# Context blocks after the latent-key blocks, low parts on VectorE, finished maps parked in DRAM

## The chip, the cores and the metric

The kernel runs on one core of a Trainium2 chip. The metric is the device time of one execution in microseconds (us). Five engines work side by side: TensorE (PE, with its weight loads as PEld), VectorE (DVE), ScalarE (ACT), GpSimd (POOL) and SyncE (SP), which here does nothing but issue DMA transfers. Each engine runs its own instructions in a fixed order, and waits on semaphores for the others. TensorE's clock has two levels, 1.2 and 2.4 GHz, shown as a granted clock of 0.5 and 1.0.

## The reference, cut to what matters

Two layers over 1024 latent tokens and 256 context tokens of width 1024, all in float32:

```
hx = modulate(rms_norm(x), ...);  hc = modulate(rms_norm(ctx), ...)
(a_q, a_k, a_v, a_g, b_cq, b_ckv, b_kr, b_g, c_u, c_v, c_g, d_b, d_c, d_h, d_g) = split(hx @ w_in)
... the same columns for hc @ w_in
out_a = neighbourhood_attention(...); out_b = latent attention over keys built from b_ckv, b_kr
out_c = spatial_gating(gelu(c_u), gelu(c_v)); out_d = short_conv(d_b, d_c, d_h)
x = x + g * (concat(out_a*silu(a_g), out_b*silu(b_g), out_c*silu(c_g), out_d*silu(d_g)) @ w_out)
```

The context tokens get the same in layer 0; in layer 1 they only give keys and values.

## The kernel before

**Numbers and tiles.** Every float32 operand of a matmul is cut into a high part (a cast) and a low part (original less high part, a subtraction), and a product is three matmuls: high by high, high by low, low by high. `split` makes both parts: the cast on ACT (L360), the subtraction on POOL unless told otherwise (L365). Tokens stand in chunks: 0 and 1 (512 latent columns each) and 2 (256 context columns). The input projection goes by blocks of 128 output columns. A weight block is a load of 512 KB on SP into a `wr` tile (L369), the cast into `wh`, the subtraction into `wl`. There are two buffers each of `wr`, `wh` and `wl`, so two weight blocks can be held at a time; `x` has 20 buffers of 512 columns, `o` has four.

**The value stage of layer 0** is `value_blocks`, between `first_groups` (two head groups, their maps finished there) and the paired projections. It runs the latent-key blocks `ckv_block(2)` and `(1)`, then the ten context blocks `ctx_first` (cq, ak, aq, bg, ag, two each, chunk 2 only, 24 matmuls of 256 columns each), then value tiles `av_tile`, and between these `ckv_block(0)`. All three latent-key blocks read the weights `w`, so from the first to the last of them one buffer of `wh` and of `wl` stays taken (wh516 and wl517 below). `pe.chain(True)` fixes TensorE's order to the order of the code; the scheduler that builds the program places the other engines' instructions.

**Strassen's operands.** Chunks 0 and 1 of the later projections go through `proj2`, seven products for what would be eight. It needs sums of the activations: `right_parts(i)` makes four additions on POOL (L693), `right_sums(i)` four differences on DVE (L700), each split again. For i of 2 and 3 the sums "3" and "4" go into `o` tiles, which hold the value weights `wav` until the last value tile `av_tile(3)`. `proj2` loads six to eight weight pieces of 256 KB into `x` tiles (L720) and splits them in `w_op`; two of its first three low parts are on POOL.

**Layer 1** is `paired`: blocks ak0, `ckv_block(2)`, `(1)`, `(0)`, a gate, ak1, the value tiles, then nine `proj2` (cg, dc, dh, db, dg, cq, ak, aq, bg and ag behind).

**After the projections** keys and queries that were written to DRAM (`scr_...`) are read back on POOL's queue and attention runs. The maps (`map_(fc, c)`, `x` tiles) are gated head outputs; numbers 4 to 7 are finished early, wait out attention in SBUF, and are read when the output is merged.

Of the kernel before, what the change touches and what calls it, by code (L numbers as in the profile page):

```python
# [13 lines left out]
ALU = mybir.AluOpType  # L14
# [5 lines left out]
SEQ = 1024  # L20
CTX = 256
TOK = SEQ + CTX
# [74 lines left out]
def backbone(ctx: ExitStack, tc: tile.TileContext, a, yT, dbg=None):  # L97
# [85 lines left out]
    def f(ap):  # L183
        return ap.bitcast(F32)
# [170 lines left out]
                dve.tensor_scalar(m["G"][:, fb, :nc_], pc[:, i, :nc_], v[:, V_BM + 16 + fb:V_BM + 17 + fb], None, ALU.add)  # L355


    def split(hi, lo, raw, hi_eng="act", lo_eng="pool"):
        if hi_eng == "act":
            act.copy(hi, raw)  # L360
        elif hi_eng == "pool":
            pool.tensor_scalar(hi, raw, 1.0, None, ALU.mult)  # L362
        else:
            dve.tensor_copy(hi, raw)
        (pool if lo_eng == "pool" else dve).tensor_tensor(lo, raw, f(hi), ALU.subtract)  # L365

    def w_load(src):
        raw = T("wr", [1024])
# [3 lines left out]
    def w_block(src, scale=None, raw=None, **k):  # L372
        if raw is None:
            raw = w_load(src)
        hi, lo = T("wh", [1024], F32R), T("wl", [1024], F32R)
        if scale is None:
            split(hi, lo, raw, **k)
        else:
            act.activation(hi, raw, AF.Copy, scale=scale)
            dve.scalar_tensor_tensor(lo, raw, scale, f(hi), ALU.mult, ALU.subtract)  # L380
        return hi.rearrange("p (k n) -> p k n", k=8), lo.rearrange("p (k n) -> p k n", k=8)
# [40 lines left out]
    def layer(l, H):  # L422
        last = l == DEPTH - 1
        v = vecs[l]
# [6 lines left out]
        def htok(t, kc, hl):  # L431
# [7 lines left out]

        scr = {k: dr.tile(s, F32, name=f"scr_{k}{l}", tag=f"scr_{k}{l}") for k, s in  # L440
               (("cq", [2, 256, TOK]), ("ck", [2, 128, TOK]), ("kr", [2, 64, TOK]), ("k", [2, 256, TOK]),
                ("q", [2, 256, TOK]), ("v", [TOK, 256]), ("vw", [4, 512, 256]))}

        M = {}

        def map_(fc, c):

            if c < 2:
                if (fc, c) not in M:
                    M[fc, c] = T("x", [512])  # L450
                return M[fc, c]
            if (fc // 2, 2) not in M:
                M[fc // 2, 2] = T("x", [2, 256])
            return M[fc // 2, 2][:, fc % 2, :]

        all_chunks = (0, 1, 2) if not last else (0, 1)

# [74 lines left out]
        ahead_w = {}  # L532
# [155 lines left out]
        def right_parts(i):  # L688

            t = {}  # L690
            for k, (c, kc) in enumerate(((0, i), (1, i), (1, i + 4), (0, i + 4))):
                t[k] = T("x", [512])
                pool.tensor_tensor(t[k], f(H[c, kc][:, 0, :]), f(H[c, kc][:, 1, :]), ALU.add)  # L693
            R["11", i], R["21", i], R["22", i] = H[0, i], H[0, i + 4], H[1, i + 4]
            return t

# [65 lines left out]
            step(6, x_, "4", False)  # L762
            evac(0, x_, 1)

        def block_c(name, c, evac):

            hi, lo = ahead_w.get(name) or w_block(a["wtb"][l, BLOCKS.index(name)])
            p = PS("b", [CHUNKS[c][1]])
            mm3(p, [(hi[:, kc, :], lo[:, kc, :], hap(c, kc, 0), hap(c, kc, 1)) for kc in range(KC)])
            evac(c, p)  # L770
# [38 lines left out]
        def value_blocks(ctx_first):  # L809

            wav = w_tok(a["wav"][l], 288, ("o", "o"), ("o", "o"))
            pe.chain(True)
            late = []

            def ckv_block(c, hi, lo):
                p = PS("b", [CHUNKS[c][1]])
                mm3(p, [(hi[:, kc, :], lo[:, kc, :], hap(c, kc, 0), hap(c, kc, 1)) for kc in range(KC)])
                late.append(ckv_steps(c, p))

            def on():  # L820
                for fn in [fns.pop(0) for fns in late if fns]:
                    fn()

            w = w_block(a["wtb"][l, BLOCKS.index("ckv0")])
            ckv_block(2, *w)
            ckv_block(1, *w)
            for name, fn in ctx_first:
                block_c(name, 2, fn)
                on()
            for t in (8, 9):  # L830
                av_tile(t, wav)
            ckv_block(0, *w)
            parts = [right_parts(0), right_parts(1)]
            for i in range(2):
                right_sums(i, parts[i])
            for t in (4, 5, 6, 7):
                av_tile(t, wav)
                on()
            for i in range(2, 4):
                right_sums(i, right_parts(i))  # L840
            for t in range(4):
                av_tile(t, wav)
            pe.chain(False)
            av_windows()

        def half_paired():
            first_groups()
            while fillers:
                fillers.pop(0)()
            evacs = {"cq": cq_evac, "ak": k_evac, "aq": lambda c, p, j: q_evac(c, p, j, 0.125),  # L850
                     "bg": lambda c, p, j: act.activation(map_(2 + j, c), p, AF.Silu),
                     "ag": lambda c, p, j: act.activation(map_(j, c), p, AF.Silu)}
            value_blocks([(f"{n}{j}", lambda c, p, n=n, j=j: evacs[n](c, p, j)) for n in evacs for j in range(2)])
            proj2("cq", evacs["cq"])
            kr = kr_rotate()
            proj2("ak", k_evac)
            kr_transpose(*kr)
            proj2("aq", evacs["aq"])
            cq_stats()
            w_tags.remove("wr")  # L860
            proj2("bg", evacs["bg"])

        def paired():
            wav = w_tok(a["wav"][l], 288, ("o", "o"), ("o", "o"))
            pe.chain(True)
            block_c("ak0", 2, lambda c, p: k_evac(c, p, 0))
            late = []

            def ckv_block(c, hi, lo):
                p = PS("b", [CHUNKS[c][1]])  # L870
                mm3(p, [(hi[:, kc, :], lo[:, kc, :], hap(c, kc, 0), hap(c, kc, 1)) for kc in range(KC)])
                for fn in [fns.pop(0) for fns in late if fns]:
                    fn()
                late.append(ckv_steps(c, p))

            w = ahead_w["ckv0"]
            ckv_block(2, *w)
            ckv_block(1, *w)
            ckv_block(0, *w)
            cv_gate(0)  # L880
            parts = [right_parts(0)]
            block_c("ak1", 2, lambda c, p: k_evac(c, p, 1))
            for fns in late[1:]:
                fns.pop(0)()
            av_tile(8, wav)
            late[-1].pop()()
            parts.append(right_parts(1))
            for t in (9, 4):
                av_tile(t, wav)
            cv_gate(1)  # L890
            for i in range(2):
                right_sums(i, parts[i])
            for t in (5, 6, 7):
                av_tile(t, wav)
            for i in range(2, 4):
                right_sums(i, right_parts(i))
            for t in range(4):
                av_tile(t, wav)
            pe.chain(False)
            av_windows()  # L900
            proj2("cg", lambda c, p, j: gate(c, p, 4 + j))
            proj2("dc", lambda c, p, j: act.copy(map_(6 + j, c), p))
            kr = kr_rotate()
            z = {}

            def conv_in(c, p, j):
                z[j, c] = T("x", [512])
                dve.tensor_tensor(z[j, c], p, map_(6 + j, c), ALU.mult)

            proj2("dh", conv_in)  # L910
            kr_transpose(*kr)
            for j in range(2):
                w = [v[:, V_SC + 3 * j + i:V_SC + 3 * j + i + 1] for i in range(3)]
                for c in range(2):
                    m = map_(6 + j, c)
                    act.activation(m, z[j, c], AF.Copy, scale=w[1])
                    for d, s_, k in ((m[:, 1:], z[j, c][:, :511], 0), (m[:, :511], z[j, c][:, 1:], 2),
                                     (m[:, 0:1], z[j, 0][:, 511:], 0) if c else (m[:, 511:], z[j, 1][:, 0:1], 2)):
                        dve.scalar_tensor_tensor(d, s_, w[k], d, ALU.mult, ALU.add)

            def mulb(c, p, j):
                m = map_(6 + j, c)
                dve.tensor_tensor(m, p, m, ALU.mult)

            proj2("db", mulb)
            proj2("dg", lambda c, p, j: gate(c, p, 6 + j))
            proj2("cq", cq_evac)
            proj2("ak", k_evac)
            proj2("aq", lambda c, p, j: q_evac(c, p, j, 0.125))
            cq_stats()  # L930
            w_tags.remove("wr")
            proj2("bg", lambda c, p, j: act.activation(map_(2 + j, c), p, AF.Silu))
# [543 lines left out]
        units[0].prep()  # L1476
        pe.chain(False)
        ph.close()
        ph = Phase("att", ("pt", "pc"))
        queue, ends = [], []  # L1480
        for u, un in enumerate(units):
# [203 lines left out]
```

## Time and profile before

| | |
|---|---|
| median of three runs | 1534.22 us (1533.8 to 1536.93) |
| the profiled execution, its own time | 1531.37 us |
| its span in the trace | 1529.6 us |
| TensorE busy | 1404.1 us, 92% of the span |
| VectorE, ScalarE, GpSimd busy | 947.6, 645.2, 567.6 us |
| moved by DMA | 171.70 MB, mean 112 GB/s |

The busy times of the engines lie side by side; with TensorE at 92% what can be gained or lost is where TensorE stands still or runs at its lower clock. Durations below come from this one execution.

### The profile page before, as it was taken

What the parts mean: (1) busy time and instruction counts of PE and PEld (TensorE: products, weight loads), DVE (VectorE), ACT (ScalarE), POOL (GpSimd) and SP (SyncE); (2) the same over time, 40 slices, a digit from 0 to 9 for tenths busy, and PEclk for the clock granted to TensorE, in tenths of its full rate; (3) what the DMA queues carried; (4) which work ended last, traced back from release to release, by engine and by line L of the source; (5) the groups of instructions that cost most, each with busy time, mean ns of one, the idle gap of its engine ahead of it and who ended that gap; (6) DMA issues with size and microseconds to landing.
All of it is one profiled execution on the core that took longest, in us unless ns stands there. A gap on an engine that the chain in (4) does not pass through costs nothing. (4 is left out here: it accounts for less than half of the span.)

```text
span 1529.6 us, 23255 instructions
## 1 busy us (share of the span) xinstructions
PE 1404.1 (92%) x8784; PEld 1176.0 (77%) x8784; DVE 947.6 (62%) x1999; ACT 645.2 (42%) x1438; POOL 567.6 (37%) x449
## 2 busy tenths in 40 slices
PE   4999999669899899999999979899999899999997
PEld 2888888559687687778888969777787678778887
DVE  5857886254554777666446564838364677765564
ACT  5612012223344666655334322433334566654543
POOL 2153354374425000245551175643434101055651
PEclk9999999769899999999999989999999999999999
DMA  9513445302457200585343112412245503285232
GB/s 354 194 49 125 138 124 176 122 20 86 165 170 171 27 1 22 134 176 144 126 151 126 57 37 81 149 46 69 69 152 154 108 1 76 80 176 144 91 129 74
DMA packets 86703, 171.70 MB, mean 112 GB/s; under 512 B 8768, under 2 KB 35392, under 8 KB 86464
## 3 DMA queue, kind: packets, MB, share of 16 engines
q1 hardware_dynamic: 69568, 141.91, 28.4%
q0 software_dynamic: 15936, 27.27, 9.2%
q8 instruction: 69, 1.13, 0.3%
q10 hardware_dynamic: 1088, 1.05, 0.2%
q14 instruction: 42, 0.34, 0.1%
HBM read 140.57 MB, written 33.82 MB: 114 GB/s over the span
## 5 line engine op out<-in xcount | busy, mean ns | idle before, releaser
L173 PE MATMUL psb<-g,wh 128*128 128x512 f32 (+1 forms) x1886 | 510.1, 371 | 16.6 <-ACT wh L360 11.1
L173 PE MATMUL psb<-g,wl 128*128 128x512 f32 (+1 forms) x1144 | 373.4, 379 | 44.3 <-POOL wl L365 36.2
L173 PEld LDWEIGHTS psb<-g,wh 128*128 128x128 f32 x1886 | 346.0, 197 | 83.0 <-ACT wh L360 14.2
L173 PEld LDWEIGHTS psb<-g,wl 128*128 128x128 f32 x1144 | 224.8, 197 | 87.5 <-POOL wl L365 39.1
L173 PE MATMUL psb<-g,st 128*128 128x512 f32 (+1 forms) x600 | 159.6, 383 | 10.4 <-ACT wl L1105 3.7
L365 POOL TENSOR_TENSOR wl<-wr,wh 128x1024 fp32r<-128x1024 f32 (+1 forms) x46 | 111.5, 2425 | 149.1 <-ACT wh L360 147.9
L1088 DVE TENSOR_REDUCE s<-psb 128x1 f32<-128x512 f32 (+1 forms) x200 | 117.5, 590 | 64.5 <-PE psb L173 62.4
L173 PE MATMUL psb<-g,g 128*128 128x256 f32 (+1 forms) x784 | 129.5, 305 | 1.8 <-ACT wh L1105 1.1
L173 PEld LDWEIGHTS psb<-g,st 128*128 128x128 f32 x600 | 95.4, 192 | 35.2 <-ACT g L1105 6.5
L173 PE MATMUL psv<-pt,g 128*64 128x256 f32 (+1 forms) x1312 | 119.4, 331 | 0.6 <-ACT pt L979 0.5
L979 ACT COPY pt<-pst 128x512 f32<-128x512 f32 x116 | 67.9, 585 | 109.5 <-PE pst L176 107.9
L173 PEld LDWEIGHTS psb<-g,g 128*128 128x128 f32 x784 | 105.4, 191 | 9.0 <-issue 2.9
L340 DVE CUSTOM_DVE_ANT_0 tmp<-g,x 128x512 f32<-128x512 f32 x112 | 96.8, 915 | 13.5 <-POOL x L474 11.8
L173 PE MATMUL psb<-g,wr 128*128 128x512 f32 (+1 forms) x490 | 98.1, 346 | 6.9 <-DMA g<-scr_cq 2.7
L173 PEld LDWEIGHTS psv<-pt,g 128*64 128x64 f32 x1312 | 79.3, 137 | 32.5 <-issue 8.6
L173 PEld LDWEIGHTS psb<-g,wr 128*128 128x128 f32 x490 | 76.9, 190 | 20.0 <-ACT wr L360 3.9
L360 ACT CAST wh<-wr 128x1024 fp32r<-128x1024 f32 (+1 forms) x41 | 40.3, 985 | 117.0 <-PE psb L173 67.9
L176 PE MATMUL pst<-ident,g 128*128 128x128 f32 x448 | 79.1, 278 | 11.3 <-ACT g L1235 6.4
L362 POOL TENSOR_SCALAR wh<-wr 128x1024 fp32r<-128x1024 f32 x16 | 44.3, 2772 | 113.1 <-PE pst L176 53.1
L977 DVE COPY pt<-pst 128x512 f32<-128x512 f32 x116 | 79.1, 683 | 6.6 <-PE pst L176 6.1
L1421 DVE SCALAR_TENSOR_TENSOR x<-psb,modG,x 128x512 f32<-128x512 f32 (+1 forms) x48 | 29.5, 615 | 85.2 <-PE psb L173 45.6
L176 PEld LDWEIGHTS pst<-ident,g 128*128 128x128 f32 x448 | 54.1, 140 | 28.0 <-ACT g L1235 8.3
(249 smaller groups left out, 2370.3 us busy)
## 6 DMA issues: line engine op xcount, KB each, us to landing
g<-in_wmod SPq DMA_DIRECT2D x48, 512.0 KB, 4.6
x<-in_wtb SPq DMA_DIRECT2D x60, 256.0 KB, 3.8
wr<-in_wtb SPq DMA_DIRECT2D x28, 512.0 KB, 3.8
wr<-in_wout SPq DMA_DIRECT2D x27, 512.0 KB, 3.6
st<-in_nab SPq DMA_DIRECT2D x24, 384.0 KB, 3.5
x<-in_xT SPq DMA_DIRECT2D x32, 256.0 KB, 5.8
g<-scr_q POOLq DMA_DIRECT2D x32, 256.0 KB, 7.3
x<-x SPq DMA_DIRECT2D x24, 256.0 KB, 2.6
```

Source lines behind the costliest of these rows:

```text
L173: return self._next(nc.tensor.matmul(*p, **k))
L176: return self._next(nc.tensor.transpose(*p, **k))
L340: dve.tensor_tensor_reduce(junk, w[:, hf * 512:hf * 512 + 512], crow[cond, hf], 1.0, 0.0, ALU.mult, ALU.add, part[:, i, cond, hf:hf + 1])
L360: act.copy(hi, raw)
L362: pool.tensor_scalar(hi, raw, 1.0, None, ALU.mult)
L365: (pool if lo_eng == "pool" else dve).tensor_tensor(lo, raw, f(hi), ALU.subtract)
L977: dve.tensor_copy(dst, src)
L979: act.copy(dst, src)
L1088: dve.reduce_max(st["mx"][:, i:i + 1], s_, AX.X)
L1421: dve.scalar_tensor_tensor(xa, p, mod[l]["G"][:, fb, cond:cond + 1], xa, ALU.mult, ALU.add)
```

## The change

In layer 0's value stage `ckv_block(0)` moves ahead of the ten context blocks; the low parts of seven of these go to DVE (two of three, the third stays on POOL); an `on()` behind the value tiles 4 to 7 goes. In layer 1 the low part of ak1 goes to DVE. `right_parts`' additions on POOL are ordered behind the last low part that the code has put on POOL so far. In both layers the finished maps 4 to 7, chunks 0 and 1, are written to DRAM (`park`, 8 transfers of 256 KB) and read back ahead of attention (`unpark`, on SP), which leaves their `x` tiles to the paired projections. The diff, cut:

```diff
     def split(hi, lo, raw, hi_eng="act", lo_eng="pool"):
...
-        (pool if lo_eng == "pool" else dve).tensor_tensor(lo, raw, f(hi), ALU.subtract)
+        m = (pool if lo_eng == "pool" else dve).tensor_tensor(lo, raw, f(hi), ALU.subtract)
+        if lo_eng == "pool":
+            last_split[0] = m
...
+        def park(fcs):
+            for fc in fcs:
+                for c in range(2):
+                    sp.dma_start(scr["m"][fc - 4, :, c * 512:(c + 1) * 512], M.pop((fc, c)))
+        def unpark():
+            for c in range(2):
+                for fc in range(4, 8):
+                    sp.dma_start(map_(fc, c), scr["m"][fc - 4, :, c * 512:(c + 1) * 512])
...
-                pool.tensor_tensor(t[k], f(H[c, kc][:, 0, :]), f(H[c, kc][:, 1, :]), ALU.add)
+                after(pool.tensor_tensor(t[k], f(H[c, kc][:, 0, :]), f(H[c, kc][:, 1, :]), ALU.add), last_split[0])
...
             ckv_block(2, *w)
             ckv_block(1, *w)
-            for name, fn in ctx_first:
-                block_c(name, 2, fn)
+            ckv_block(0, *w)
+            for n, (name, fn) in enumerate(ctx_first):
+                block_c(name, 2, fn, lo_eng=("dve", "pool")[n % 3 == 2])
                 on()
             for t in (8, 9):
                 av_tile(t, wav)
-            ckv_block(0, *w)
...
             for t in (4, 5, 6, 7):
                 av_tile(t, wav)
-                on()
...
             first_groups()
             while fillers:
                 fillers.pop(0)()
+            park((4, 5, 6, 7))
...
-            block_c("ak1", 2, lambda c, p: k_evac(c, p, 1))
+            block_c("ak1", 2, lambda c, p: k_evac(c, p, 1), lo_eng="dve")
...
             proj2("cg", lambda c, p, j: gate(c, p, 4 + j))
+            park((4, 5))
...
             proj2("dg", lambda c, p, j: gate(c, p, 6 + j))
+            park((6, 7))
...
         ph.close()
+        unpark()
```

The first place is POOL in layer 0's context blocks. In a row stand the number, the line, the operation, the tile written and those read; `wl` from a `wr` is a low part of a weight block, `x` from `g` an addition of `right_parts`, `s` a reciprocal square root. Before:

```order
66 L365 TENSOR_TENSOR wl536_2618<-wr534_2615,wh535_2617 128x1024
67 L218 TENSOR_TENSOR s540_2653<-s521_2537,mhalf_3_73 128x2
68 L218 TENSOR_TENSOR s545_2668<-s525_2567,mhalf_3_73 128x4
69 L365 TENSOR_TENSOR wl552_2688<-wr550_2685,wh551_2687 128x1024
70 L606 TENSOR_TENSOR x530_2599<-x530_2599,tmp538_2646 128x256
71 L365 TENSOR_TENSOR wl557_2723<-wr555_2720,wh556_2722 128x1024
72 L365 TENSOR_TENSOR wl562_2758<-wr560_2755,wh561_2757 128x1024
...
82 L693 TENSOR_TENSOR x603_3057<-g91_302 128x512
83 L693 TENSOR_TENSOR x604_3059<-g142_469 128x512
84 L365 TENSOR_TENSOR wl588_2930<-wr586_2927,wh587_2929 128x1024
```

and after:

```order
65 L367 TENSOR_TENSOR wl562_2750<-wr560_2747,wh561_2749 128x1024
66 L218 TENSOR_TENSOR s545_2698<-s521_2546,mhalf_3_73 128x2
67 L218 TENSOR_TENSOR s550_2713<-s525_2576,mhalf_3_73 128x4
68 L622 TENSOR_TENSOR x534_2638<-x534_2638,tmp543_2691 128x256
69 L218 TENSOR_TENSOR s555_2730<-s529_2606,mhalf_3_73 128x4
70 L367 TENSOR_TENSOR wl578_2857<-wr576_2854,wh577_2856 128x1024
71 L367 TENSOR_TENSOR wl593_2959<-wr591_2956,wh592_2958 128x1024
72 L709 TENSOR_TENSOR x604_3079<-g67_227 128x512
```

Ten low parts have become three, and no addition stands ahead of the last of them (wl588 before, wl593 after).

The second place is POOL at the end of layer 0's value stage. `o` from `x` is the low part of a sum "3" or "4"; wh658 and wl659 are low parts of the first two weight operands of `proj2("cq")`. Before:

```order
94 L693 TENSOR_TENSOR x637_3260<-g125_408 128x512
95 L365 TENSOR_TENSOR g613_3092<-x605_3061,g613_3092 128x512
96 L693 TENSOR_TENSOR x638_3262<-g159_530 128x512
97 L218 TENSOR_TENSOR s619_3159<-s597_3046,mhalf_3_73 128x4
98 L693 TENSOR_TENSOR x639_3264<-g157_525 128x512
99 L365 TENSOR_TENSOR wh658_3412<-x652_3402,wh658_3412 128x512
100 L365 TENSOR_TENSOR wl659_3415<-x653_3404,wl659_3415 128x512
101 L365 TENSOR_TENSOR o633_3247<-x629_3236,o633_3247 128x512
102 L365 TENSOR_TENSOR o635_3255<-x631_3240,o635_3255 128x512
```

and after:

```order
88 L367 TENSOR_TENSOR o633_3256<-x629_3245,o633_3256 128x512
89 L367 TENSOR_TENSOR o635_3264<-x631_3249,o635_3264 128x512
90 L709 TENSOR_TENSOR x636_3267<-g123_403 128x512
91 L709 TENSOR_TENSOR x637_3269<-g125_408 128x512
92 L709 TENSOR_TENSOR x638_3271<-g159_530 128x512
93 L709 TENSOR_TENSOR x639_3273<-g157_525 128x512
94 L367 TENSOR_TENSOR wh658_3421<-x652_3411,wh658_3421 128x512
95 L367 TENSOR_TENSOR wl659_3424<-x653_3413,wl659_3424 128x512
96 L367 TENSOR_TENSOR wh661_3434<-x654_3415,wh661_3434 128x512
```

The two low parts into `o` tiles now stand ahead of the four additions of `right_parts(3)`, and these ahead of the weights' low parts. Layer 1 ends its value stage in the same new order.

The third place is POOL at the start of layer 1's value stage; wl1914 (after: wl1922) is the low part of the weights of the latent-key blocks, `o` from `wr` one of `wav`. Before:

```order
224 L218 TENSOR_TENSOR s1902_8709<-s1901_8707,mhalf_3_73 128x16
225 L693 TENSOR_TENSOR x1965_9132<-g1763_7904 128x512
226 L693 TENSOR_TENSOR x1966_9134<-g1844_8395 128x512
...
236 L693 TENSOR_TENSOR x2016_9459<-g1775_7934 128x512
237 L365 TENSOR_TENSOR wl1914_8781<-wr1912_8778,wh1913_8780 128x1024
238 L365 TENSOR_TENSOR o1933_8945<-wr1935_8950,o1932_8944 128x576
```

and after:

```order
217 L218 TENSOR_TENSOR s1910_8735<-s1909_8733,mhalf_3_73 128x16
218 L367 TENSOR_TENSOR wl1922_8807<-wr1920_8804,wh1921_8806 128x1024
219 L367 TENSOR_TENSOR o1941_8971<-wr1943_8976,o1940_8970 128x576
220 L367 TENSOR_TENSOR o1945_8981<-wr1946_8982,o1944_8980 128x576
221 L367 TENSOR_TENSOR o1945_8981<-wr1947_8986,o1944_8980 128x576
222 L709 TENSOR_TENSOR x1973_9158<-g1771_7929 128x512
```

The twelve additions ahead of the latent keys' low part are gone from there; eight stand behind the last low part of `wav`.

## Rows read from the trace of the kernel before

**Rows 1.** The page: busy time of each engine, instructions

```profile
PE 1404.1 (92%) x8784; PEld 1176.0 (77%) x8784; DVE 947.6 (62%) x1999; ACT 645.2 (42%) x1438; POOL 567.6 (37%) x449
```

**Rows 2.** Windows: busy time (count) by engine, clock, DMA share, GB/s

```profile
core 0: us, PE busy (x) PEld busy (x) DVE busy (x) ACT busy (x) POOL busy (x), PEclk, DMA share, GB/s
250.00:260.40 10.40, 10.40 (x66) 9.34 (x65) 5.18 (x13) 2.59 (x6) 3.66 (x2) 1.00 0.15 50
260.40:337.00 76.60, 46.49 (x240) 42.70 (x239) 25.23 (x27) 16.60 (x29) 39.14 (x22) 0.71 0.25 79
```

**Rows 3.** Groups by line in 260.4 to 337: mean ns, idle before, releaser

```profile
L173 PE MATMUL psb<-g,wl 128*128 128x256 f32 x73 | 28.5, 390 | 22.5 <-POOL wl L365 22.5
L365 POOL TENSOR_TENSOR wl<-wr,wh 128x1024 fp32r<-128x1024 f32 x9 | 21.6, 2395 | 43.7 <-ACT wh L360 43.7
L360 ACT CAST wh<-wr 128x1024 fp32r<-128x1024 f32 x9 | 9.4, 1044 | 49.0 <-PE psb L173 22.1 <-issue 20.6 <-POOL x L693 6.4
```

**Rows 4.** Waits of TensorE in 260.4 to 337: total, times, longest

```profile
PE psb L173 <- POOL wl L365: 22.5, 9, 7.4
PE psb L173 <- ACT wh L360: 7.6, 8, 1.1
```

**Rows 5.** Timeline of POOL there: start, us, operation

```profile
319.12 10.45 POOL L693 TENSOR_TENSOR x<-g 128x512 f32<-128x512 f32 x7
329.52 2.80 POOL L365 TENSOR_TENSOR wl<-wr,wh 128x1024 fp32r<-128x1024 f32 x1
```

**Rows 6.** Timeline of TensorE: ckv_block(0) between value tiles

```profile
343.05 0.62 PE L173 MATMUL psb<-g,wh 128*128 128x512 f32 x2
...
348.62 2.56 PE L173 MATMUL psb<-o,g 128*128 128x288 f32 x18
```

**Rows 7.** The page: weight block loads, KB each, us to landing

```profile
wr<-in_wtb SPq DMA_DIRECT2D x28, 512.0 KB, 3.8
```

**Rows 8.** Line L365: low parts by engine, ns min/median/max

```profile
L365 DVE TENSOR_TENSOR g<-x,g x16: 677/684/2829, 325.3 to 975.9; 128x512 fp32r<-128x512 f32 x16
L365 POOL TENSOR_TENSOR o<-x,o x8: 1287/1517/1789, 375.8 to 986.1; 128x512 fp32r<-128x512 f32 x8
L365 DVE TENSOR_TENSOR wl<-wr,wh x7: 1214/1222/1226, 778.1 to 841.0; 128x1024 fp32r<-128x1024 f32 x7
```

**Rows 9.** Timeline at the value stage's end, layer 0: POOL, then TensorE

```profile
366.96 1.28 POOL L365 TENSOR_TENSOR wh<-x,wh 128x512 fp32r<-128x512 f32 x1 [2.57 <-ACT wh L360]
375.81 5.50 POOL L365 TENSOR_TENSOR o<-x,o 128x512 fp32r<-128x512 f32 x4 [5.63 <-ACT o L360]
...
376.64 2.94 PE L173 MATMUL psb<-g,wh 128*128 128x512 f32 x12
379.42 2.96 PE L173 MATMUL psb<-g,wl 128*128 128x512 f32 x12
```

**Rows 10.** TensorE's longest stop in layer 0's paired projections, and the clock after

```profile
403.98 1.22 PE L173 MATMUL psb<-g,wl 128*128 128x512 f32 x2 [5.64 <-ACT wl L360]
...
400.75:411.00 10.25, 6.35 (x18) 4.86 (x19) 0.85 (x2) 1.85 (x3) 7.27 (x13) 0.50 0.53 171
```

**Rows 11.** Layer 1, value stage's start: POOL, TensorE, window

```profile
897.59 16.80 POOL L693 TENSOR_TENSOR x<-g 128x512 f32<-128x512 f32 x12
914.35 2.33 POOL L365 TENSOR_TENSOR wl<-wr,wh 128x1024 fp32r<-128x1024 f32 x1
...
916.74 0.58 PE L173 MATMUL psb<-g,wl 128*128 128x256 f32 x1 [9.96 <-POOL wl L365]
...
909.33:919.57 10.24, 2.83 (x13) 2.83 (x14) 0.62 (x2) 0.07 (x1) 10.24 (x8) 0.50 0.22 60
```

**Rows 12.** Layer 1, first paired projection: TensorE's two stops, POOL, window

```profile
983.26 3.06 PE L173 MATMUL psb<-g,wr 128*128 128x512 f32 x12 [1.07 <-ACT tmp L742]
990.36 5.53 PE L173 MATMUL psb<-g,wl 128*128 128x512 f32 x16 [3.10 <-POOL wl L365]
...
982.19:995.00 12.81, 8.64 (x29) 6.61 (x30) 6.04 (x7) 6.20 (x11) 10.59 (x8) 0.87 0.73 240
```

**Rows 13.** DMA at the turn to attention: windows, and layer 1's key loads

```profile
480.00:500.00 20.00, 19.12 (x96) 15.61 (x95) 10.96 (x20) 9.01 (x16) 12.40 (x19) 1.00 1.45 293
1180.00:1200.00 20.00, 15.78 (x69) 12.49 (x68) 7.88 (x13) 6.71 (x11) 7.95 (x12) 0.90 1.45 263
...
g<-scr_cq POOLq DMA_DIRECT2D x4, 512.0 KB, 12.8
```

More of the change, by code (lines that the diff above doesn't have):

```diff
@@ L355, in mod_store @@
                 dve.tensor_scalar(m["G"][:, fb, :nc_], pc[:, i, :nc_], v[:, V_BM + 16 + fb:V_BM + 17 + fb], None, ALU.add)
+    last_split = [None]
     def split(hi, lo, raw, hi_eng="act", lo_eng="pool"):
@@ L441, in layer @@
                (("cq", [2, 256, TOK]), ("ck", [2, 128, TOK]), ("kr", [2, 64, TOK]), ("k", [2, 256, TOK]),
-                ("q", [2, 256, TOK]), ("v", [TOK, 256]), ("vw", [4, 512, 256]))}
+                ("q", [2, 256, TOK]), ("v", [TOK, 256]), ("vw", [4, 512, 256]),
+                ("m", [4, 128, SEQ]))}
         M = {}
@@ L763, in proj2, with block_c @@
             evac(0, x_, 1)
-        def block_c(name, c, evac):
-            hi, lo = ahead_w.get(name) or w_block(a["wtb"][l, BLOCKS.index(name)])
+        def block_c(name, c, evac, **k):
+            hi, lo = ahead_w.get(name) or w_block(a["wtb"][l, BLOCKS.index(name)], **k)
             p = PS("b", [CHUNKS[c][1]])
```

## The prediction

> **What bounds the kernel now.** I read the page first: TensorE is busy 1404.1 of 1529.6 us, 92% [rows 1]. No other engine comes near, so only the stretches in which TensorE stands still or has its lower clock can pay. Second, windows by stage. Just ahead of the context blocks TensorE is busy without a break at a granted clock of 1.00; from 260.4 to 337 it is busy 46.49 of 76.60 us at 0.71 [rows 2]. That is the worst stretch of the program by far. Third, what it waits for there: 22.5 us for the low parts on POOL and 7.6 for the casts on ACT, nine and eight times [rows 4]. The casts wait in turn for TensorE (22.1 us of ACT's idle time) [rows 3]. So the ten blocks go in a ring: with wh516 and wl517 taken until `ckv_block(0)`, one buffer pair is left; a cast (1.04) can start when TensorE has read the block before, then comes the low part (2.40), and TensorE mostly waits. Fourth, the same look at the other places that the change moves: the ends of the two value stages, the start of layer 1's, the turn to attention.
>
> **The change part by part.**
>
> *Layer 0's context blocks.* Before, ten blocks take 76.6 us, and `ckv_block(0)` later 348.62 - 343.05 = 5.6 [rows 2, 6]: 82.2 together. After, `ckv_block(0)` directly follows its sisters at 5.6, and the ten blocks have two buffer pairs. A lower bound for them is TensorE's own work at full clock: 24 matmuls of 256 columns, half of the 24 of 512 columns that took 5.6, so at least 2.8; I use 3.1 for the first few at a block's start and the small sums between, 31 for ten. The upper one is the ring that is left: a `wr` buffer is free when its low part is done, so every second block needs load 3.8 [rows 7], cast 1.04, and low part 1.22 on DVE [rows 8] or 2.40 on POOL [rows 3]: 6.1 to 7.2 for two blocks, some 36 for ten with signals between. The two bounds lie close. I take 33 (loads of the first blocks are there in time, as TensorE works more than 11 us on two latent-key blocks of 5.6 ahead of them). Saving 82.2 - 5.6 - 33 = 43.6; bounds 40.6 and 45.6. The last stop, 7.4 us in [rows 4], goes with it: seven additions of 10.45 us stood ahead of the low part on POOL [rows 5], and none does now. DVE, which gets seven low parts of 1.22, has 25.23 us of work in the stretch of 76.60 [rows 2]; in 38.6 us it would be some 34 busy, and behind each low part stand the differences that empty the block before, so it is close to filled but holds.
>
> What DVE's part costs beside POOL is the open point. The 16 low parts of 512 columns on DVE have a median of 0.684 us and a longest of 2.829 [rows 8]; the seven of 1024 columns, at 778 to 841 us, all took 1.22. If DVE's were stretched by as much as POOL's own takes here (1.2 us each, for the blocks next to one of POOL's three), 3 to 4 of them would cost up to 4 us, which is the end of the range I use, not the value. The Trainium skill (SBUF — State Buffer, "Who interferes with whom") says that a VectorE instruction with two SBUF inputs and a GpSimd one that reads SBUF can't run together: the second blocks until the first is done. By it the 2.829 above is a wait and no slower run, and the saving would be some 40 in place of 43.6; no row shows the pair in these blocks.
>
> *The end of layer 0's value stage.* Before, POOL was done with the first weights' low parts at 368, TensorE left the last value tile at 376.64 and went through two products without a stop, while POOL made the four `o` low parts behind them (5.50) [rows 9]. After, the order on POOL is: two `o` low parts, four additions, then the first weight's low part. The `o` tiles come free only as `av_tile(3)` reads `wav` for the last time, about 1.6 us ahead of its end; a cast of 0.6 follows. Counted from the end of `av_tile(3)`: the low parts run from -1 to +1.8 (1.4 to 1.5 each, 5.50 for four), the additions at 1.40 to 1.49 ([rows 5, 11]) to +7.5, the weight's low part at 1.28 [rows 9] to +8.8. TensorE has only high-part products until then, six of about 0.25 (2.94 for twelve), 1.5 us. So it stands about 7.3 us. A stop of this size is followed by the lower clock: after the 5.64 at 398 the clock was 0.50 for 10.25 us with TensorE busy 6.35 of them [rows 10], half of which is lost, 3.2. Together 10.5. Bounds: 6 (additions partly early, no clock loss), 14.
>
> *Layer 1's start.* TensorE stands 9.96 us for the latent keys' low part, because POOL made twelve additions, 16.80 us, ahead of it; then it is 2.83 busy at 0.50, 1.4 lost [rows 11]. After, no addition is ahead: 11.4 saved. Against it, eight additions now stand ahead of the small `s` operations of the latent keys' norm, whose result the order of TensorE waits for: 8 x 1.40 = 11 us, of which TensorE covers most with `ckv_block(1)`, `(0)`, the gate and ak1; I take 2 back (0 to 5). Saving 9.4.
>
> *Layer 1's value stage end.* The same new order, so the same 10.5. It takes the place of what stood there: 1.07 and 3.10 of stop [rows 12] and, with a clock of 0.87 over 12.81 us there, about 1.7 more: 5.9. Loss 4.6.
>
> *Parking.* 8 transfers of 256 KB out and 8 in, per layer. The writes stand on SP behind the gates and ahead of loads that are early anyway; I cost them at nothing, cover being TensorE's 10 us of unbroken work [rows 2]. If a weight load is held by them it is one landing, 3.8 [rows 7]. The reads go out next to the loads of keys and queries, where the DMA engines are over-full (share 1.45, 263 to 293 GB/s) [rows 13]. In layer 1 the maps were free early and most are read ahead of that; in layer 0 about 1 MB falls into it. 1 MB at 293 GB/s is 3.6 us of DMA time; TensorE was busy 19.12 of 20 us there, so I take 1 for both layers, range 0 to 7 (2.1 MB at 293, once).
>
> *The sum.* 43.6 - 10.5 + 9.4 - 4.6 - 1 = 36.9 less; by the tighter ends of the clock and DVE terms 33, so I take 36. The profiled execution's own 1531.4 gives 1495.4. It lay 2.85 under the median of the runs; the changed kernel's median should lie as far above its profile, so 1498.
>
> **The rivals.** (a) *No stop at the value stages' ends.* If POOL's additions were early enough, the 10.5 of layer 0 and the 4.6 of layer 1 (there even the 5.9 of before would go) are not lost: 1498 - 10.5 - 10.5 = 1477 at best, 1484 with half of it. Against it speaks the order: the additions are tied behind low parts that need `o` tiles. (b) *Loads and DVE bind the blocks.* The ring at 36 and DVE's wait at 4 take 3 + 4, the turn to attention 6 more, the stops at 14 in place of 10.5 twice 7: 1498 + 20 = 1518 with all, 1508 with half. (c) *Slower than before.* One mechanism: POOL's chain in the value stages. It has 16 additions of 1.49 and 8 low parts of 1.52, 36 us, all of it now behind the ten blocks, and the value tiles last only 376.6 - 337 - 5.6 = 34 us [rows 2, 6, 9]. At these durations 24 us of it lie ahead of the last tile's end, which leaves 10 free. Beside DVE's 16 differences, each could take up to twice as long (2.829 against 0.684 is more than that [rows 8]); then 72 us stand against 34 and TensorE would stop 38 in place of 7.3 in layer 0, and about 20 in layer 1: 1498 + 31 + 13 = 1542. It decides from about 1.9 times the durations on. The rows at 319 and 897, taken with DVE beside them, show 1.49 and 1.40. (d) *The change doesn't do what it says*: the blocks' ring stays, as the slots would be held by something else. The order shows three low parts on POOL in place of ten, so little is left of this; only the 9.4 of layer 1 less 15 would remain: about 1540.
>
> **How the numbers follow.** Forecast 0.60 (1490 to 1506), (a) 0.12, (b) 0.20, (c) 0.03, (d) 0.01, and 0.04 for a gain under 0.2% by several small losses, mostly at the turn to attention. A measurement of this kernel can tell about 0.2%, 3 us, from no change. The range leaves out (c), (d), and the far halves of (a) and (b): 1483 to 1514. Faster 0.92, same 0.04, slower 0.04.
>
> **What would show it.** In the trace after: the ten context blocks within 31 to 37 us at a clock near 1.00, starts of casts some 3.3 us apart; DVE's low parts there at 1.22, or stretched to over 2 (the blocks' term is then too high); behind `av_tile(3)` in both layers a stop of TensorE of 6 to 9 us that ends with a POOL low part, and the lower clock behind it; in layer 1 no stop of 10 us ahead of `ckv_block(2)`; the stretch before attention no longer than before by more than 4 us. The prediction is wrong if the blocks still go at 5 us or more each, or if the stop behind the value tiles is under 2 us or over 15.

## The result, and the profile after

The changed kernel takes 1511.65 us (median of 4 runs, 1507.57 to 1513.84) against 1535.58 (1533.8 to 1540.26): a ratio of 0.984, interval 0.980 to 0.987. It is 24 us faster; 36 were forecast. The time lies inside the stated range (1483 to 1514), near its upper end, and outside the 1490 to 1506 that the prediction gave its own sum.

The profiled execution took 1513.53 us, 1.9 above its median, while that of before lay 4.2 under the median of the runs that are now known. So the two traces differ by 17.9 us of span only (1529.6 to 1511.7), and the stages below add up to that within 0.2. The page after; the first line answers to [rows 1]:

```profile
PE 1402.0 (93%) x8784; PEld 1173.9 (78%) x8784; DVE 947.7 (63%) x2007; ACT 646.0 (43%) x1438; POOL 552.1 (37%) x441
```

TensorE has the same 8784 matmuls and is busy 2 us less; the rest is time in which it stood. The stage lengths, read from the starts of the same matmuls in both traces (us; the end of `ckv_block(1)` is at 257.6 before and 260.2 after):

| stretch | before | after | change | predicted |
|---|---|---|---|---|
| start to the end of `ckv_block(1)`, layer 0 | 257.6 | 260.2 | +2.6 | 0 |
| to the last value tile, layer 0 | 118.9 | 80.4 | -38.5 | -43.6 |
| into the fourth paired projection, layer 0 | 88.9 | 102.1 | +13.2 | +10.5 |
| to layer 1 | 421.1 | 422.1 | +1.0 | +1 |
| to layer 1's last value tile | 87.6 | 83.2 | -4.4 | -9.4 |
| into the fourth paired projection, layer 1 | 81.6 | 89.0 | +7.4 | +4.6 |
| to the end | 474.0 | 474.6 | +0.6 | 0 |

Every predicted move has its sign, and four of them came out worse than their size by 2.7 to 5.1 us. The 2.6 of the first stretch are no effect of the change: executions differ there by up to 4 us (last section).

**The context blocks, after.** The windows of the ten blocks, and of the half-clock stretch in them (columns as in [rows 2]):

```profile
265.80:308.80 43.00, 35.95 (x271) 34.49 (x270) 17.91 (x32) 15.90 (x27) 17.58 (x11) 0.92 0.47 154
277.54:284.37 6.83, 5.82 (x27) 5.47 (x28) 3.07 (x7) 1.24 (x2) 0.14 (x1) 0.50 0.60 220
```

What TensorE waited for in the ten blocks (total, times, longest; the answer to [rows 4]):

```profile
PE pst L176 <- DVE s L223: 4.4, 2, 3.5
PE psb L173 <- DVE wl L367: 1.2, 2, 0.8
PE psb L173 <- ACT wh L362: 0.9, 1, 0.9
PE psb L173 <- POOL wl L367: 0.4, 1, 0.4
```

The 30 us of waiting for low parts and casts [rows 4] have become 2.5. What is left is new: 4.4 us for L223, the last step of the latent keys' reciprocal square root, and a stretch at half clock that starts as the longer of the two stops ends. The chain that makes L223 is short operations that go from POOL (L218) to DVE (L220, L221, L223) to TensorE, and they stand behind longer ones: on DVE behind a low part, on POOL behind L622. The timeline of POOL, DVE and TensorE:

```profile
269.92 2.37 POOL L367 TENSOR_TENSOR wl<-wr,wh 128x1024 fp32r<-128x1024 f32 x1 [15.07 <-ACT wh L362]
275.23 1.48 POOL L622 TENSOR_TENSOR x<-x,tmp 128x256 f32<-128x256 f32 x1 [1.26 <-ACT tmp L616]
276.67 1.01 POOL L218 TENSOR_TENSOR s<-s,mhalf 128x4 f32<-128x4 f32 x1
...
274.90 1.23 DVE L367 TENSOR_TENSOR wl<-wr,wh 128x1024 fp32r<-128x1024 f32 x1 [0.25 <-ACT wh L362]
...
277.61 1.08 PE L176 MATMUL pst<-ident,s 128*128 128x128 f32 x4 [3.49 <-DVE s L223]
```

Before, the ring was so slow (some 8 us a block, and a step after each) that this chain was never late: TensorE came to its next step 6.7 us after the sums (261.7 to 268.4). Now it comes 3 us after them (270.7 to 273.7), and there are three chains in place of two.

**The end of layer 0's value stage, after.** TensorE, POOL, DVE, ACT and SP behind the last value tile, which ends at 341 (the answer to [rows 9]):

```profile
342.12 0.72 PE L173 MATMUL psb<-g,wh 128*128 128x512 f32 x2 [1.16 <-ACT wh L362]
350.75 0.80 PE L173 MATMUL psb<-g,wh 128*128 128x512 f32 x1 [7.26 <-ACT wh L362]
...
342.43 5.39 POOL L709 TENSOR_TENSOR x<-g 128x512 f32<-128x512 f32 x4
347.78 1.71 POOL L367 TENSOR_TENSOR wh<-x,wh 128x512 fp32r<-128x512 f32 x1
...
345.18 1.51 DVE L740 TENSOR_TENSOR x<-x,x 128x512 f32<-128x512 f32 x1 [3.54 <-DMA x<-in_wtb]
346.62 1.75 DVE L716 TENSOR_TENSOR x<-x,x 128x512 f32<-128x512 f32 x1
348.29 1.75 DVE L741 TENSOR_TENSOR x<-x,x 128x512 f32<-128x512 f32 x1
...
350.07 0.62 ACT L362 CAST wh<-x 128x512 fp32r<-128x512 f32 x1 [1.05 <-DVE x L741]
...
341.86 0.88 SPq L736 DMA_DIRECT2D x<-in_wtb  x2
```

The window of the half clock, which starts within the longer stop:

```profile
345.81:356.05 10.24, 5.30 (x13) 4.15 (x14) 10.24 (x8) 3.08 (x5) 8.67 (x6) 0.50 0.48 173
```

The stop is 8.4 us (1.16 and 7.26), the four additions are where the order put them, and the lower clock lasts 5.3 us beyond the stop. But the last to come is not the first weight's low part, as I had said (done at 349.5): it is the third weight's cast, 1.2 us later. Its chain starts with a load that stands on SP behind the last value tile's spill and lands at 345.1. On DVE it takes an addition (L740, 1.51) and a difference (L741, 1.75), with a difference of `right_sums` (L716, 1.75) between them, all beside POOL.

**Layer 1, after.** The start, then the value stage's end (the answers to [rows 11] and [rows 12]):

```profile
886.01 12.07 POOL L709 TENSOR_TENSOR x<-g 128x512 f32<-128x512 f32 x8
898.04 2.91 POOL L218 TENSOR_TENSOR s<-s,mhalf 128x16 f32<-128x16 f32 x1
900.98 0.17 DVE L220 SCALAR_TENSOR_TENSOR s<-s,s 128x16 f32<-128x16 f32 x1 [11.20 <-POOL s L218]
901.72 1.66 POOL L218 TENSOR_TENSOR s<-s,mhalf 128x2 f32<-128x2 f32 x1 [0.77 <-DVE s L598]
904.03 0.69 PE L176 MATMUL pst<-ident,s 128*128 128x128 f32 x2 [4.59 <-DVE s L223]
...
952.59 0.72 PE L173 MATMUL psb<-g,wh 128*128 128x512 f32 x2 [4.21 <-ACT wh L362]
959.48 0.80 PE L173 MATMUL psb<-g,wh 128*128 128x512 f32 x1 [5.15 <-ACT wh L362]
```

The stop of 9.96 is gone, and one of 4.59 stands in its place, for the latent keys' chain. It stands behind more than the eight additions: the power of 128x16 is the gate's norm, whose steps come first on POOL and on DVE, and only then goes the latent keys' power of 128x2. At the end 9.4 us of stop are where 4.2 were.

### The profile page after: what moved, and what is told of

It reads as the page before. It is cut to its first block, busy times and chain, and to the rows that moved or that the text cites. A ratio compares the mean times of both kernels' runs of the same rounds, so it can differ in the third digit from the quotient of the medians.

```text
span 1511.7 us, 23317 instructions
## 1 busy us (share of the span) xinstructions
PE 1402.0 (93%) x8784; PEld 1173.9 (78%) x8784; DVE 947.7 (63%) x2007; ACT 646.0 (43%) x1438; POOL 552.1 (37%) x441
## 4 chain that ended last, share of the span: by engine, by line
PE 75%; DVE 6%; issue 5%; DMA 5%; POOL 4%; ACT 3%; SPq 1%; DVEq 0%; ACTq 0%; POOLq 0%
PE psb L173 59%; PE psv L173 7%; PE pst L176 7%; PE pst L173 1%; DMA x<-in_wtb 1%; DMA wr<-in_wtb 1%; POOL s L218 1%; POOL x L709 1%; DVE x L716 1%; DVE s L1106 1%; DMA g<-scr_cq 1%; POOL wl L367 1%; DVE pt L995 1%; ACT g L1253 1%; DMA wr<-in_wav 1%
## 5 line engine op out<-in xcount | busy, mean ns | idle before, releaser
L173 PEld LDWEIGHTS psb<-g,wh 128*128 128x128 f32 x1886 | 341.1, 193 | 92.7 <-ACT wh L362 24.6
L173 PE MATMUL psb<-g,wl 128*128 128x512 f32 (+1 forms) x1144 | 369.4, 375 | 11.9 <-ACT wl L362 7.3
L173 PEld LDWEIGHTS psb<-g,wl 128*128 128x128 f32 x1144 | 219.7, 193 | 55.2 <-ACT wl L362 9.4
L367 POOL TENSOR_TENSOR wl<-wr,wh 128x1024 fp32r<-128x1024 f32 (+1 forms) x38 | 92.9, 2445 | 137.3 <-ACT wh L362 136.1
L340 DVE CUSTOM_DVE_ANT_0 tmp<-g,x 128x512 f32<-128x512 f32 x112 | 92.5, 876 | 13.4 <-POOL x L490 11.2
L173 PEld LDWEIGHTS psb<-g,wr 128*128 128x128 f32 x490 | 77.5, 190 | 17.9 <-ACT wr L362 3.7
```

The lines of the kernel that those rows point to most:

```text
L173: return self._next(nc.tensor.matmul(*p, **k))
L340: dve.tensor_tensor_reduce(junk, w[:, hf * 512:hf * 512 + 512], crow[cond, hf], 1.0, 0.0, ALU.mult, ALU.add, part[:, i, cond, hf:hf + 1])
L367: m = (pool if lo_eng == "pool" else dve).tensor_tensor(lo, raw, f(hi), ALU.subtract)
```

## The experiments

The theory after the traces: (1) the move of `ckv_block(0)` gives the gain, through the second buffer pair; (2) the new order of POOL's additions takes part of it back behind both last value tiles; (3) the latent keys' chain takes another part, in the blocks and at layer 1's start; (4) parking and VectorE's low parts matter little. The stage lengths of all kernels, read as above, each from one profiled execution (us; "blocks" from the end of `ckv_block(1)` to the first value tile, and a part of the column behind it):

| kernel | blocks | to last tile, layer 0 | paired, layer 0 | to last tile, layer 1 | paired, layer 1 | median |
|---|---|---|---|---|---|---|
| before | 79.0 | 118.9 | 88.9 | 87.6 | 81.6 | 1535 |
| after | 48.6 | 80.4 | 102.1 | 83.2 | 89.0 | 1511.7 |
| e1 no order | 49.7 | 81.6 | 91.0 | 88.6 | 79.9 | 1501.9 |
| e2 no parking | 48.2 | 80.1 | 101.0 | 83.0 | 88.6 | 1508.3 |
| e3 no move | 63.7 | 106.1 | 101.4 | 84.5 | 88.5 | 1533.8 |
| e4 low parts on POOL | 50.2 | 82.1 | 99.1 | 82.7 | 88.5 | 1514.4 |
| e5 additions ahead | 49.5 | 81.4 | 91.8 | 83.5 | 87.7 | 1506.6 |
| e6 chain later | 40.9 | 72.8 | 101.2 | 79.9 | 87.9 | 1501.1 |
| e7 both, loads early | 42.6 | 74.4 | 94.2 | 79.9 | 89.6 | 1495.6 |
| e8 next loads too | 41.9 | 73.8 | 91.6 | 78.4 | 87.9 | 1490.0 |
| e9 the move alone | 50.8 | 82.6 | 98.2 | 88.5 | 82.8 | 1509.0 |
| e10 layer 1's additions | 41.8 | 73.7 | 91.8 | 78.4 | 87.8 | 1491.0 |

In the kernels without the move, `ckv_block(0)` lies in the second column and not in the first. The stretches that the table leaves out explain a part of the medians: the one to layer 1 takes 421 to 424 us in all kernels but e1 (427.7) and e5 (428.1), which lose these 6 us at the turn to attention, with two stretches of half clock at some 487 and 504 us that the changed kernel does not have there. Why was not looked for. The last one takes 470.4 (e1) to 477.3 us (e4).

**e1, no order of the additions.**

```diff
-                after(pool.tensor_tensor(t[k], ..., ALU.add), last_split[0])
+                pool.tensor_tensor(t[k], ..., ALU.add)
```

> The changed kernel without the order of right_parts' additions behind the last low part on POOL. Theory A (that order makes the stop of 8.4 us of TensorE behind layer 0's last value tile, and of 9.4 us behind layer 1's): POOL's additions for i = 3 come ahead of the low parts into the o tiles again, the stop behind layer 0's value tiles falls below 3 us, the same in layer 1, while in layer 1 the twelve additions again stand ahead of the latent keys' low part and the stop of about 10 us returns in place of the 4.6 us one. Layer 0 gains some 10, layer 1 gains 7 and loses 5: about 1500. Rival B (the last load of the first weights, which stands on SP behind the last value tile's spill, ends the stop, not POOL): the stop behind layer 0's value tiles stays at 6 us or more, and with layer 1's lost start the kernel is the same or slower, 1512 to 1518.

1501.9 us (1497.42 to 1509.44), ratio to before 0.981 (0.976 to 0.985). Theory A holds in layer 0: POOL makes fifteen additions in one row and TensorE passes into the first products with a stop of 1.10. From the timeline, POOL and TensorE:

```profile
303.54 25.18 POOL L709 TENSOR_TENSOR x<-g 128x512 f32<-128x512 f32 x15
...
343.15 3.05 PE L173 MATMUL psb<-g,wh 128*128 128x512 f32 x12 [1.10 <-DVE tmp L572]
```

That is 11.1 us of the 13.2 that the change lost there. The late load, rival B, can have only a small part: in the changed kernel the first weight's low part, done at 349.5 behind the additions, would alone have held TensorE to within 1.2 us of the end of its stop. This run doesn't separate the two further, as its last load goes out earlier too (337.8 in place of 341.9). In layer 1 the old stop is back (10.0 us for the low part) and the new one is gone: 5.4 lost at the start, 9.1 won at the end.

**e2, no parking.** Without the calls of `park` and `unpark`.

> The changed kernel without parking: the maps 4 to 7 stay in SBUF. Theory A (parking neither costs nor gives): within 4 us of the changed kernel, 1508 to 1515, the stops at their places. Rival B (the tiles that parking frees are what lets the paired projections' weights come in time): slower by 5 to 15 us, with new stops of TensorE for loads in the paired projections, 1517 to 1527. Rival C (the extra traffic collides with the key and query loads): faster by 2 to 6 us, with the gain at the turn to attention.

1508.34 us (1507.02 to 1510.47), ratio 0.984 (0.982 to 0.986): theory A. No stage differs from the changed kernel's by more than 1.1 us. In this kernel the freed tiles are not used for anything that was late.

**e3, no move.** `ckv_block(0)` back behind the value tiles 8 and 9, with its calls of `on()`.

> The changed kernel with ckv_block(0) back behind the first two value tiles, the low parts still mostly on VectorE. Theory A (the second buffer pair is what shortens the ten blocks): the ring of one pair remains, with cast 1.04, low part 1.22 and TensorE's 2.9: 5.5 us for a block with VectorE, 6.6 with POOL, and more where the clock falls, 58 to 65 us for ten in place of the 41 of the changed kernel: slower by 17 to 25, about 1530. Rival B (VectorE's shorter low part is what counts): 41 to 48 us for ten, slower by less than 8.

1533.82 us (1531.94 to 1538.41), ratio 1.000 (0.999 to 1.002): the whole gain is gone, as theory A says. The ring is faster than before, 63.7 for ten blocks as expected, but what TensorE waits for (its waits from 261 to 325 us) is the same list as in [rows 4], with part of POOL's place taken by DVE:

```profile
PE psb L173 <- ACT wh L362: 7.4, 8, 1.1
PE psb L173 <- POOL wl L367: 5.9, 3, 2.0
PE psb L173 <- DVE wl L367: 5.1, 6, 1.6
```

The 12.8 us that VectorE's low parts and the additions' later place win together here are lost again behind the last value tile (101.4 against 88.9); by e1 that is the price of the order.

**e4, all ten low parts on POOL.**

```diff
-                block_c(name, 2, fn, lo_eng=("dve", "pool")[n % 3 == 2])
+                block_c(name, 2, fn, lo_eng="pool")
```

> The changed kernel with all ten low parts of the context blocks in layer 0 on POOL. Theory A (with two buffer pairs the low part's engine matters little, as load 3.8, cast 1.04 and low part 2.40 make 7.2 us for two blocks, 36 for ten): slower by 2 to 6 us. Rival B (POOL's low parts of 2.40 delay the latent keys' norm chain on POOL as well, and the clock falls): slower by 10 to 20 us.

1514.4 us (1513.02 to 1516.2): 1.6 in the blocks and 2.7 in the median, theory A. With two buffer pairs, and with the order of the additions kept, the low part's engine is nearly free to choose.

**e5, both sets of additions ahead of the sums.**

```diff
-            for i in range(2, 4):
-                right_sums(i, right_parts(i))
+            ps = [right_parts(2), right_parts(3)]
+            for i in range(2, 4):
+                right_sums(i, ps[i - 2])
```

> The changed kernel, the order of the additions behind the low parts kept, but in both layers right_parts(2) and right_parts(3) are both called ahead of right_sums(2): no addition stands behind a low part that waits for an o tile. Theory A (only the additions' place behind the o low parts makes the stops behind the value tiles): the stretch from the last value tile to the fourth paired product falls from 100.7 to about 90 us in layer 0, layer 1's from 84.5 to about 80, the start of layer 1 stays as it is: about 1497. Rival B (the removal of the order itself is what helped, as the additions run during the context blocks): layer 0's stop stays above 4 us, gain under 5 us.

1506.6 us (1502.33 to 1508.12). Layer 0 as expected (91.8): there the place behind the `o` low parts makes the stop, and the order itself does no harm. Layer 1 not: 87.7 in place of 80. There the eight additions of `right_parts(2)` and `(3)` now start behind the low parts of the sums before them, 8 us ahead of the tiles' end. DVE's differences beside them take 1.75 us each, and behind these stands the copy of a value tile's last columns, which TensorE waits for (timelines of POOL, DVE and TensorE):

```profile
937.25 12.25 POOL L709 TENSOR_TENSOR x<-g 128x512 f32<-128x512 f32 x8
953.32 0.18 DVE L572 COPY tmp<-psb 128x32 f32<-128x32 f32 x1
953.64 5.05 PE L173 MATMUL psb<-g,wh 128*128 128x512 f32 x12 [6.97 <-DVE tmp L572]
```

The median misses the 1497 expected by 9.6; beside layer 1's end, the stretch to layer 1 (6.0 longer than in the changed kernel, above) has part in that.

**e6, the chain later.** Layer 0: `on()` only behind the first and fourth context block. Layer 1: `right_parts(0)` and `(1)` called behind the chain, and ordered behind its last power.

> The changed kernel with the latent keys' norm chain given more time. Layer 0: its steps are called after the first and the fourth context block, not after the first and the second. Layer 1: right_parts(0) and (1) are both made behind the chain, ordered behind its last power on POOL. Theory A (TensorE's stops of 3.49 and 0.94 in the context blocks and 4.59 in layer 1, each with lower clock behind it, are that chain's latency and POOL's queue): the value stage of layer 0 falls from 76.5 to about 69, that of layer 1 from 87.7 to about 81, together 13 us: about 1498. Rival B (the clock falls there anyway, or the chain's place only moves the stop): under 5 us.

1501.11 us (1498.33 to 1501.75), ratio 0.978 (0.976 to 0.980). Layer 0's blocks: 7.7 us less, and the window has the clock that I had assumed for the change:

```profile
265.00:300.30 35.30, 32.82 (x271) 31.93 (x270) 18.32 (x32) 15.99 (x27) 16.83 (x11) 1.00 0.57 187
```

and TensorE's waits in it are two:

```profile
PE psb L173 <- POOL wl L369: 1.2, 1, 1.2
PE psb L173 <- DVE wl L369: 1.2, 2, 0.8
```

Layer 1 gains 3.3 of the 6 to 7 that I expected; a stop of 2.1 stays, now for a copy on DVE. The chain is a cause in both layers, rival B falls.

**e7, both together, and the first loads early.** e5 and e6, and the weights of the first paired projection loaded ahead of the last four value tiles.

> The two changes of the kernels before this one together (additions ahead of the sums, chain later), and the first paired projection's weight loads issued ahead of the last four value tiles. If the gains add: 10 + 4 in the stops behind the value tiles, 7 + 6 in the chain, about 1485. If the loads were a limit too, TensorE passes from the value tiles to the first product without any stop and the clock stays at 1.00 until the stop for the second projection's weights.

1495.58 us (1495.05 to 1496.36), ratio 0.975 (0.973 to 0.976). The gains of the medians add (5.1 in e5, 10.5 in e6, 16.1 here); the 1485 expected counted on 14 us behind the value tiles, which e5 alone had not given. In layer 0 TensorE still stops 2.7 us behind the tiles, for a copy on DVE, so the loads were not all that stood there (94.2 against 91.8 in e5); in layer 1 the pairing's start is no better than in the changed kernel.

**e8, the next loads too.** As e7, and in layer 0 the weights of ak are loaded ahead of the first projection's products, into tiles that parking left free.

> As the kernel before this one, and in layer 0 the second paired projection's weights (ak) are loaded ahead of the first one's, into the tiles that parking left free; before they stand on SP behind the first one's spills. Theory A (the stop of 5.4 us in the second projection, and the lower clock of 10 us behind it, is that load's lateness): gone, 5.4 and about 5 of clock, some 10 us: about 1475. Rival B (another wait takes its place, as VectorE and POOL have the splits of both projections at once): under 4 us.

1489.98 us (1488.87 to 1497.45), ratio 0.973 (0.970 to 0.976): the fastest kernel here. The median falls by 5.6; the gain over e7 is 2.6 in layer 0's pairing, where I had expected 10: the stop of 6.9 us there (5.4 in the changed kernel) became one of 4.36 at the same place, and the half clock behind it stays. Rival B. Whether these loads could be had without parking was not tried.

**e9, the move alone.** The kernel before with `ckv_block(0)` moved and the one `on()` dropped; no order, no VectorE, no parking.

> The kernel before with the move of ckv_block(0) (and the dropped call behind the value tiles) alone: low parts on POOL, no order of the additions, no parking. Theory A (the move is the gain, VectorE's low parts give about 2 us and the order of the additions takes some 10 back): layer 0's value stage about 78 us in place of 116.2, no stop of 7 us behind it, layer 1 as before: about 1498, faster than the whole change by 10 or more. Rival B (the low parts and the order are needed to get the move's gain): 1510 or more, with seven additions ahead of a low part as before.

1508.97 us (1502.94 to 1512.56), ratio 0.983 (0.979 to 0.987): not to be told from the whole change. So the move carries it, and the other parts cancel. But I had expected 1498, with no stop of 7 us behind the value stage. There are stops of 1.89 and 2.91 us there and the paired stage takes 98.2: POOL, with ten low parts ahead, makes additions until 340.9 (332.1 in e1), and the differences on DVE and two weight loads come late behind them. e1, which has VectorE's low parts and parking beyond this one, takes 91.0. The 7.2 us thus belong to these two together. Most of it should be VectorE's low parts, as they free POOL; but the two loads wait on SP, 2.4 and 1.5 us, for work on `x` tiles by the profile, and such tiles are what parking frees; e2 shows parking to be idle only where the order makes the stop. The two were not taken apart.

**e10, layer 1's additions in another order.** As e8, with `right_parts(0)` to `(2)` behind the chain and `(3)` behind the first sums.

> The kernel e8 with layer 1's additions in another order: right_parts(0) to (2) right behind the latent keys' chain, (3) behind the first sums, so that fewer additions lie in the last value tiles. Theory A (the stop of 6.96 us behind layer 1's value tiles is VectorE's copy of the rotary key, queued behind differences that wait for POOL's eight additions): that stop falls below 2 us and the lower clock of 6.8 us behind it goes, 8 us less: about 1482. Rival B (VectorE is held up by POOL's work as such, as it takes 1.75 us a difference beside POOL against 0.68 alone, wherever the additions stand): the stop only moves, under 3 us.

1490.99 us (1489.54 to 1493.97), against 1489.98: rival B. Both layer 1 stages stay within 0.1. The stop of 6.96 at the last tile's end became two, 3.60 and 5.44, the second for the copy of a finished product (timeline of TensorE):

```profile
931.73 3.73 PE L173 MATMUL psb<-g,wh 128*128 128x512 f32 x10 [3.60 <-POOL wh L369]
946.44 2.07 PE L173 MATMUL psb<-g,wr 128*128 128x512 f32 x4 [5.44 <-ACT tmp L767]
```

## Why the prediction was right, and where it was too high

**The blocks (-43.6 forecast, -38.5).** The mechanism was right: e9 and e3 show that the move gives the gain and that without it there is none. Two sizes were off. The one before was a slip of mine: the window of 76.6 us holds nine casts and nine waits, as [rows 3] and [rows 4] say; the tenth block, with its weights at hand, ran ahead of it. All ten took 79.0. The one after was the miss that counts: 43.0 in place of 33. I had bounded it by TensorE's work and the `wr` ring only. The small steps that `on()` runs between the blocks appear in my sum as "small sums", at no wait. With the blocks at 3 us they are a chain of POOL, DVE and TensorE that is too long; e6 puts it elsewhere and gets 35.3 at full clock. So the chain's 7.7 were missing, and 2.3 more lay in the 33: TensorE alone is busy 32.8 there, where I had counted 31. The value tiles behind came out 2.5 shorter, for which there was no term; with the 2.4 more of before and the 10.0 more of after that makes the 38.5. The rule for such a place: where the turn of a ring falls from 7.9 us to 3.5, whatever is called once a turn has that much less time.

**DVE beside POOL in the blocks (0, up to 4).** The low parts on DVE were not stretched: POOL's three stand between them and seldom beside them. The group of the line in the ten blocks:

```profile
L367 DVE TENSOR_TENSOR wl<-wr,wh 128x1024 fp32r<-128x1024 f32 x6 | 7.6, 1259 | 24.3 <-ACT wh L362 24.3
```

The contention that I had put here came elsewhere, at the stages' ends: 1.75 for a difference beside POOL, 0.68 alone, and POOL's low parts of 512 columns 1.71 where 1.28 was read [rows 9]. There each of the two engines ends an operation every 1.7 us, in turn: a pair takes 1.7, nearly the 0.68 and 1.28 of the two alone added up (1.96). The Trainium skill (SBUF — State Buffer, "Who interferes with whom") has it so: of a VectorE instruction with two inputs in SBUF, the on-chip memory, and a GpSimd one that reads SBUF the second to issue blocks until the first is done. This trace agrees, but for the 0.3 by which a pair is shorter than the sum.

**Behind the value tiles (+10.5 each time; +13.2 and 89.0 - 81.6 = +7.4 net, where +4.6 was forecast).** The order was read rightly and the cause holds in layer 0 (e1, e5). The stop of 7.3 was 8.4, since the low parts and differences took 1.7 each beside one another and since the third weight's chain, which I had not followed (late load, an addition and a difference on DVE, cast), came last. The lower clock cost about as forecast: busy 5.30 us at 0.50 there, 2.7 lost. The rest, some 2 us, lies in longer stops and half clock at the second projection. In layer 1 the cause is wider than I said: e5 takes the additions from behind the `o` low parts and wins 1.3 only, e10 moves them again and wins nothing. By e5's trace what binds there is POOL's and DVE's two-input work, by turns, of which more is left than the last value tiles cover; e1, where POOL's additions are done before these tiles, takes 79.9. No run takes that work away, so the cause in layer 1 is read from traces and not shown by a run of its own. It was rival (c)'s mechanism, at a smaller price.

**Layer 1's start (-9.4; -4.4).** The 9.96 went, as said. I took 2 back for the chain behind eight additions, with a range to 5; it was 4.59 of stop, and 6.83 us at half clock with TensorE busy 4.98 of them, 2.5 lost: 7.1, which leaves 4.3 of the 11.4. The clock that goes with a stop was counted in the other terms and forgotten in this one, and so was the gate's norm ahead of the chain.

**Parking (+1; 1.7).** About as forecast: against e2 the changed kernel's stretch to layer 1 is 0.7 longer and its last one 1.0.

**The profile against the median.** I moved the sum by 2.85 us, by which the profiled execution lay under the median. The changed kernel's lay above its own. The step was worth nothing: single executions of one program differ by as much (below).

**The rivals.** The sum's own range, 1490 to 1506, did not hold; the time lies where only rival (b)'s nearer half had widened it. (b) was nearest: its time for half of its terms was 1508, but mostly by other terms: of its four, the stops (13.2 in layer 0, where it had 14) and a slower ring (35.3 in e6, where it had 36) are seen, DVE's wait and the turn to attention are not. What made up the miss, the latent keys' chain, stood in no term. That the time fell into the range is in part luck. (d) and (a) fall by the trace; (c) showed in layer 1 and in e9, at 2 to 7 us and not at 44.

## What to carry to other kernels

When a wait is taken out of a ring, list what runs once a turn and was early, above all short operations that pass between engines: their time per turn shrinks with the ring. An order edge that keeps one engine's bulk work out of the way is paid where that work ends; look at what stands behind it at the next change of stage before it is added, and cost every stop with the clock behind it. And where a change has five parts, the part that frees the buffer may carry it alone: here it gives 26 us alone, and the whole change 24.

## What the runs showed of the hardware

The start differs from execution to execution though TensorE's work there is the same: the 607th matmul began at 104.3 us at the earliest and 108.4 at the latest in the twelve traces, in the two of e2 and of the changed kernel. So much of a difference of two profiles says nothing on a change.

VectorE and GpSimd, each with two inputs in SBUF, took turns: 1.75 us in place of 0.68 on the one, 1.71 in place of 1.28 on the other, an operation of each every 1.7. At the ends of the value stages this makes their work nearly a sum, where I had put it side by side.
